# Two transformer blocks on one core: the FFN's norm weight behind the transposes, the modulation blocks placed anew

## The chip, the cores and the metric

The kernel runs on one core of a Trainium2 chip, as one launch. The metric is the device time of that launch in microseconds (us). The core has TensorE (PE, matrix products; its weight loads are listed as PEld), VectorE (DVE), ScalarE (ACT), GpSimd (POOL) and SyncE (SP), each with an instruction queue of its own that is worked through in order, and 16 DMA engines, which SP's and POOL's queues feed here.

## The reference

Two blocks over 256 tokens of width 1024, float32 throughout (cut; the mixers' insides are left out):

```python
def first_block(x, ...):
    h = rms_norm(x, norm_mix_pre)
    proj = h @ w_in
    gates = sigmoid(proj[..., SB_COLS + RW_COLS:] + b_gate)
    o_sb = stick_breaking_attention(q, k, v)
    o_rw = rwkv7_time_mix(p_rw, ...)
    merged = gates[..., :D] * (o_sb @ w_sb_out) + gates[..., D:] * (o_rw @ w_rw_out)
    x = x + rms_norm(merged @ w_o, norm_mix_post)
    h = rms_norm(x, norm_ffn_pre)              # (x * rstd(x)) * norm_ffn_pre
    f = (silu(h @ w_ffn_gate) * (h @ w_ffn_up)) @ w_ffn_down      # d_ff 2816
    return x + rms_norm(f, norm_ffn_post)

def second_block(x, c, ...):
    mod = silu(c) @ w_ada + b_ada                  # w_ada: 1024 x 6144
    sh1, sc1, g1, sh2, sc2, g2 = split(mod, 6)
    h = modulate(x, sh1, sc1)                      # rms_norm(x) * (1 + sc1) + sh1
    u, z, xbc, dt = split(h @ w_in)
    mix = concat([pool_mixer(u, ...), ssd_mixer(z, xbc, dt, ...)]) @ w_out
    x = x + g1 * mix
    h = modulate(x, sh2, sc2)
    x = x + g2 * hier_moe(h, ...)                  # 32 experts, top 2 within a group
    return rms_norm(x) * final_norm_w
```

## The kernel before

Tokens stand in two blocks of 128 (`tb` 0 and 1). Activations that feed a product stand transposed, channels on the 128 partitions, as a pair of float32r tiles: a rounded high part and the rest (`h2Th`, `h2Tl`). Weights are split the same way where they are used: ACT casts the high part (`wh`, L300), DVE subtracts it from the weight (`wl`, L301), and `mm3` (L330 to L332) makes three matmuls of one product. A block of 128 output columns over 1024 inputs (`dense_T`) is 24 matmuls of 256 columns. So each weight costs ACT a cast, DVE a subtraction and PE three matmuls, in that order.

The stages in order, with their place in the profiled span: q, k, v and RWKV's projections (to about 133 us); the gates' products (`pgate`), whose 24-matmul groups stand on PE between the attention's and RWKV's small products (`pwt`, `po`, `pz`; to about 230 us); the two mixers' output products `psb` and `prw`, gated and added into `mTh`/`mTl` (`mg`, L849 to L851); `w_o` with a norm behind it (262 to 304 us); the FFN in 22 groups `g`, each a gate block `pfg` and an up block `pfu` (to 442 us); `w_ffn_down` with two norms behind it (to 518 us); block 2's projection, SSD and pooling, `w_out`, the router (to about 657 us); the experts, whose weights SP streams from memory (to 1107 us).

`dense_rows` makes a product with tokens on the partitions: weights come as row blocks, the last few are kept split, so that token block 0 ends first; then `finish(0)` is written, the kept products of token block 1, `fill()` and `finish(1)`. What `fill` holds is independent PE work for the time in which `finish(1)` is not ready. A scheduler orders the instructions on each engine by its own estimates; the code's `tc.issue_after` can force one behind another. The engines then keep that order.

**The norm at the FFN** (`fin_mix`, L912). POOL makes `gpf` = post-norm weight times FFN-norm weight (L904) and `xgf` = x times FFN-norm weight (L908), ahead of `w_o`'s end. Behind `w_o`, ACT squares the sums `acc` (`sink`, L276), DVE multiplies `acc` by `gpf` (`pn`) and forms the row's reciprocal root in three steps of two small instructions (`rsv`, `rsy`, `rst`; L281 to L288), DVE adds both into `xgf` (L920), PE transposes that (`ptr`, 8 tiles of 128x128), and ACT and DVE take it out as `h2Th` and `h2Tl` in halves of 512 columns. `fin_mix2` makes x itself once more from `acc` (DVE L929, POOL L930), squares it, and PE spreads its reciprocal root over the partitions (`pr`, L933) as `r2`, which scales the FFN's gate products behind them.

**The modulation** `silu(c) @ w_ada` is cut into 24 blocks of 256 columns, 1 MB each, loaded on POOL's queue into two buffers (`wada`). A pair of blocks on PE (`mod_steps`) is 16 `pmod` products (the profile lists such a float32 product as two instructions), a copy of the sums on ACT (`modrow`), four transposes and two small DVE instructions. A block on DVE (`mod_late`) is one multiply and seven multiply-adds of 128x256 (`msum`), two tiny PE products (`pmc`) and an addition. Four pairs stand in the first stage, two in `w_o`'s `fill`, eight blocks on DVE in the FFN (g = 4, 6, ... 18), two pairs in `w_ffn_down`'s `fill`.

**The norms at the projection** (`fin_ffn`, L997): post-norm, addition to x, a second root, x times 1+sc1 (half on DVE, half on POOL), `diag` of the root, and 8 transposes against `diag`, with the shift sh1 added by two products of 512 columns. `fill` there is `router_prep` (L1014): `prb`, the two modulation pairs, `g2h` and `g1row` (rows of modT spread over the partitions, `row_of`, L262).

## Time and profile before

| | us |
|---|---|
| median of 3 runs | 1121.05 |
| lowest and highest | 1119.37, 1121.59 |
| the profiled execution's own time | 1120.24 |
| its span | 1118.5 |
| PE busy | 1053.5 (94%) |
| DVE busy | 592.2 (53%) |
| ACT busy | 403.6 (36%) |
| POOL busy | 82.0 (7%) |

The span is the time between the first and the last instruction of the profiled execution; the times of the runs hold 1.7 us more around it. Busy shares are means over stages with different limits. The chain of work that ended last is PE for 73% of the span, DMA for 15% and DVE for 7%. The clock that TensorE was granted is 0.987 of full speed in the mean.

### The profile page before, as it was taken

The numbers are of one execution on the slowest core, as the hardware profiler recorded it, in microseconds if no ns is written. First come the engines' busy times: TensorE is split into PE (matmuls) and PEld (weight loads), VectorE is DVE, ScalarE is ACT, GpSimd is POOL, SyncE is SP. The second block draws the span as 40 slices with busy tenths as digits, with TensorE's granted clock in tenths as the row PEclk, the third lists the DMA queues.
The fourth block names the chain that finished last, engine by engine and source line by source line (L and its number), as shares of the span: only waits on it lengthen the run. The fifth ranks groups of instructions, "written<-read, shape, count | busy, mean of one in ns | idle before, by whom it ended". The sixth has DMA issues, their size and how long they took to land.

```text
span 1118.5 us, 17553 instructions
## 1 busy us (share of the span) xinstructions
PE 1053.5 (94%) x7022; PEld 732.2 (65%) x7022; DVE 592.2 (53%) x1228; ACT 403.6 (36%) x713; POOL 82.0 (7%) x155
## 2 busy tenths in 40 slices
...
DMA  9654520256566773636664599999999999999993
GB/s 328 219 214 163 193 81 16 101 181 234 196 256 227 263 287 121 253 113 227 247 208 151 184 326 419 410 419 416 416 421 416 415 420 417 416 419 417 417 418 150
DMA packets 57717, 313.01 MB, mean 280 GB/s; under 512 B 8864, under 2 KB 11040, under 8 KB 28064
## 3 DMA queue, kind: packets, MB, share of 16 engines
...
q8 instruction: 57, 0.93, 0.3%
...
## 4 chain that ended last, share of the span: by engine, by line
PE 73%; DMA 15%; DVE 7%; ACT 2%; issue 2%; POOL 1%; SPq 0%; DVEq 0%; POOLq 0%; ACTq 0%
PE ph L1508 15%; DMA wexp<-in_w_dram 11%; PE pyo L1571 7%; PE acc L331 3%; PE acc L332 3%; PE acc L330 3%; PE moe L1589 2%; PE pga L1353 2%; DVE wl L301 2%; PE pfg L330 2%; PE pfg L331 2%; PE pfg L332 2%; PE pfu L331 2%; PE pfu L330 2%; PE pfu L332 2%
## 5 line engine op out<-in xcount | busy, mean ns | idle before, releaser
L1508 PE MATMUL ph<-wexp,xg 128*64 128x512 f32 x1024 | 229.5, 595 | 9.6 <-DMA wexp<-in_w_dram 9.0
L1508 PEld LDWEIGHTS ph<-wexp,xg 128*64 128x64 f32 x1024 | 71.8, 137 | 159.8 <-issue 129.3
L1571 PE MATMUL pyo<-wexp,gy 128*64 128x512 f32 x512 | 116.9, 599 | 2.6 <-DVE gy L1565 2.1
L1515 DVE TENSOR_TENSOR gy<-gy,ph 128x256 f32<-128x256 f32 x32 | 13.5, 421 | 152.2 <-ACT gy L1514 152.2
L1576 DVE SCALAR_TENSOR_TENSOR gy<-pyo,gs,g2h 128x512 f32<-128x512 f32 x32 | 24.0, 751 | 103.5 <-PE pyo L1571 103.5
L1571 PEld LDWEIGHTS pyo<-wexp,gy 128*64 128x64 f32 x512 | 34.1, 137 | 62.5 <-issue 53.7
L1514 ACT ACTIVATE gy<-ph 128x256 f32<-128x256 f32 x32 | 12.3, 383 | 165.0 <-PE ph L1508 165.0
L301 DVE TENSOR_TENSOR wl<-wrows,wh 128x1024 fp32r<-128x1024 f32 (+1 forms) x42 | 51.4, 1241 | 24.9 <-ACT wh L300 24.6
L301 DVE TENSOR_TENSOR wl<-wff,wh 128x1024 fp32r<-128x1024 f32 x44 | 55.1, 1253 | 17.2 <-ACT wh L300 17.1
L1580 ACT CAST yh<-gy 64x512 fp32r<-64x512 f32 x32 | 19.8, 618 | 115.6 <-DVE gy L1576 115.6
L300 ACT CAST wh<-wff 128x1024 fp32r<-128x1024 f32 x44 | 46.0, 1045 | 36.4 <-DMA wff<-in_w_ffn_dram 21.5
L300 ACT CAST wh<-wrows 128x1024 fp32r<-128x1024 f32 (+1 forms) x46 | 45.3, 1009 | 30.5 <-PE acc L331 21.7
L330 PE MATMUL pfg<-h2Th,wh 128*128 128x256 f32 x176 | 50.7, 288 | 0.1
L332 PE MATMUL pfg<-h2Th,wl 128*128 128x256 f32 x176 | 50.0, 284 | 0.0
L331 PE MATMUL pfu<-h2Tl,wh 128*128 128x256 f32 x176 | 49.9, 284 | 0.0
L330 PE MATMUL pfu<-h2Th,wh 128*128 128x256 f32 x176 | 49.9, 284 | 0.0
L332 PE MATMUL pfu<-h2Th,wl 128*128 128x256 f32 x176 | 49.9, 283 | 0.0
L331 PE MATMUL pfg<-h2Tl,wh 128*128 128x256 f32 x176 | 49.9, 283 | 0.0
L1353 PE MATMUL pga<-sel,hnh 128*128 128x256 f32 x128 | 33.1, 305 | 8.7 <-DVE sel L1347 7.0
L332 PE MATMUL pi<-h3Th,wl 128*128 128x256 f32 (+1 forms) x136 | 38.7, 284 | 1.8 <-DVE wl L301 1.8
L331 PE MATMUL pi<-h3Tl,wh 128*128 128x256 f32 (+1 forms) x136 | 38.6, 284 | 0.0
L330 PE MATMUL pi<-h3Th,wh 128*128 128x256 f32 (+1 forms) x136 | 38.6, 284 | 0.0
...
## 6 DMA issues: line engine op xcount, KB each, us to landing
...
```

Of the source, the lines that this page charges most:

```text
L300: act.copy(hi, src)
L301: eng.tensor_tensor(lo, src, hi.bitcast(F32), ALU.subtract)
L330: pe.matmul(ps, lhsT=lh, rhs=rh, start=first, stop=False)
L331: pe.matmul(ps, lhsT=lh, rhs=rl, start=False, stop=False)
L332: pe.matmul(ps, lhsT=ll, rhs=rh, start=False, stop=last)
L1353: return pe.matmul(ps, lhsT=hn[tb][part][:, k * P : (k + 1) * P], rhs=sel[tb].rearrange("p (e j s) -> p e j s", e=GE, j=2)[:, :, 0, :], st ...
L1508: last = pe.matmul(ph_[64 * t_ : 64 * t_ + 64, :], lhsT=xg[k // 4][:, (k % 4) * 256 + el * CAP : (k % 4) * 256 + el * CAP + CAP], rhs=wa[k ...
L1515: dve.tensor_tensor(g, g, ph_[:, 256:512], ALU.mult)
L1571: last = pe.matmul(py_[64 * t_ : 64 * t_ + 64, :], lhsT=gT[:, (kc % 2) * P + (kc // 2) * 64 : (kc % 2) * P + (kc // 2) * 64 + 64], rhs=wb[ ...
L1576: dve.scalar_tensor_tensor(y32, py_, gs, g2h, op0=ALU.mult, op1=ALU.mult)
L1580: act.copy(y[hi], y32[hi])
L1589: last = pe.matmul(acc[tb][hf], lhsT=sT[:, tb * P : (tb + 1) * P], rhs=ys[hf], start=(e == 0), stop=(e == E - 1))
```

## The change

**The FFN's norm weight.** `norm_ffn_pre` is no longer spread over the rows (`gffn`, a DMA on SP's queue); it stands in the table of channel parameters, and multiplies by channel (a scalar of each partition) where the transposes are taken out: ACT writes `h2Th` and DVE `h2Tl` in eight pieces of 128x128 for each token block, in the order `K_TURNS`, which the FFN's products then follow. POOL's five products (`gpf`, four `xgf`) and its four additions to x are gone; `fin_mix` makes x itself in place on DVE, so `fin_mix2` no longer makes it a second time. The 9 matmuls `warm` behind the transposes are gone.

**The order at the FFN's norm.** Three of the FFN's weight splits, of blocks (0,0), (0,1) and (1,0), are written ahead of `finish(0)`; later ones, the root of token block 1 and the first modulation block on DVE are held behind the last piece of `h2Tl` (`behind`).

**The modulation.** One pair moves from `w_o`'s `fill` into the gates' stage; the one that stays there has its products ahead and its sums inside `finish(1)`. The FFN has ten blocks on DVE (g = 3, 5, ... 21) and `w_ffn_down` two (`between`); no pair is left in `router_prep`.

**The norms at the projection.** The squares stand ahead of `pn`; token block 0's transposes are taken out only behind `diag` of token block 1; `prb` and `g2h` are only multiplied in `fill` and taken out behind both norms. `g1row` (8 float32 products of 128x128 and two ACT copies) moves into the SSD stage, behind its last `pys` products.

```diff
-WARM = (16, 4, 5, 2, 9)
+WARM = (16, 4, 5, 2)
+K_TURNS = (0, 4, 1, 5, 2, 6, 3, 7)
...
+    def behind(*ins):
+
+        st = ExitStack()
+        for i in ins:
+            st.enter_context(tc.issue_after(i.ins))
+        return st
...
-    def mod_steps():
+    def mod_products():
...
+
+        def sums():
+            row = small("modrow", [P, 512], bufs=1)
+            act.copy(row, ps)
...
+
+        return sums
+
+    def mod_steps():
+        mod_products()()
...
+        mod_left.append((i, s_))
+
+    def mod_late_sums():
+        while mod_left:
+            i, s_ = mod_left.pop(0)
             ps = psm("pmc")
...
+        if g == 0:
+            mod_steps()
...
+            if between:
+                between(n_)
         for k, hi, lo in kept:
             go(0, k, hi, lo)
+        if ahead:
+            ahead()
         finish(0, acc[0])
...
-    gffn = row_bcast("gffn", a["norm_ffn_pre"])
     h2T = act_T("h2T")
-
-
-    gpf = blk("gpf")
-    pool.tensor_tensor(gpf, gpost, gffn, ALU.mult)
-    xgf = [[hblk("xgf") for _ in range(2)] for _ in range(2)]
-    for tb in range(2):
-        for hf in range(2):
-            pool.tensor_tensor(xgf[tb][hf], halves(xr[tb])[hf], halves(gffn)[hf], ALU.mult)
...
+    def ff_split(g, j):
+
+        if g not in ff_views:
+            t = raw("wff")
+            sync.dma_start(out=t, in_=a["w_ffn"][g])
+            ff_views[g] = [t[:, i * 1024 : i * 1024 + 1024].rearrange("p (k c) -> p k c", k=KC) for i in range(2)]
+        if (g, j) not in ff_parts:
+            ff_parts[g, j] = wsplit(ff_views[g][j], P, (lambda s_: blk(s_, F32R)) if j else None)
+        return ff_parts[g, j]
+
+    def ff_ahead():
+        for gj in ((0, 0), (0, 1), (1, 0)):
+            ff_split(*gj)
...
     def fin_mix(tb, acc):
         t = blk("pn")
-        r = row_rstd(acc, EPS)
+        with behind(*last_split[0]):
+            sums = row_sums(acc)
+            for hf in range(2):
+                dve.tensor_tensor(halves(t)[hf], acc[hf], halves(gpost)[hf], ALU.mult)
+        r = row_rstd_of(sums, EPS)
+        if tb:
+            mod_o.pop()()
         for hf in range(2):
-            dve.tensor_tensor(halves(t)[hf], acc[hf], halves(gpf)[hf], ALU.mult)
-        for hf in range(2):
-            u = xgf[tb][hf]
-            dve.scalar_tensor_tensor(u, halves(t)[hf], r, u, op0=ALU.mult, op1=ALU.add)
-        last = transposed(xgf[tb], None, tb, h2T)
-        if tb:
-            warm(WARM[4], psm("warm"), last)
-        later.append((tb, acc, t, r))
-
-    def fin_mix2(tb, acc, t, r):
-        for hf in range(2):
-            x_, t_ = halves(xr[tb])[hf], halves(t)[hf]
-            dve.scalar_tensor_tensor(t_, acc[hf], r, halves(gpost)[hf], op0=ALU.mult, op1=ALU.mult)
-            pool.tensor_tensor(x_, x_, t_, ALU.add)
+            x_ = halves(xr[tb])[hf]
+            dve.scalar_tensor_tensor(x_, halves(t)[hf], r, x_, op0=ALU.mult, op1=ALU.add)
+        _, pts = transposes(halves(xr[tb]), None)
+        for k in K_TURNS:
+            src = pts[k // 4][:, k % 4 * P : k % 4 * P + P]
+            hi, lo = (atv(h2T[x], k, tb * P, tb * P + P) for x in range(2))
+            h2_done[:] = [act.activation(hi, src, AF.Copy, scale=prm("norm_ffn_pre", k)),
+                          dve.scalar_tensor_tensor(lo, src, prm("norm_ffn_pre", k), hi.bitcast(F32), op0=ALU.mult, op1=ALU.subtract)]
+        later.append(tb)
+
+    def fin_mix2(tb):
         q = row_rstd(halves(xr[tb]), EPS, eps2[:, tb : tb + 1])
         ps = psm("pr2")
         pe.matmul(ps[:, 0:P], lhsT=q.to_broadcast([P, P]), rhs=ident, start=True, stop=True)
         act.copy(r2[:, tb * P : tb * P + P], ps[:, 0:P])
...
-    dense_rows(a["w_o"], KC, mT, fin_mix, SO, keep_o, pos=PO, fill=lambda: [mod_steps() for _ in range(2)])
+    dense_rows(a["w_o"], KC, mT, fin_mix, SO, keep_o, pos=PO, ahead=ff_ahead, fill=lambda: mod_o.append(mod_products()))
...
-    total = None
     for g in range(NF):
-        t = raw("wff")
-        sync.dma_start(out=t, in_=a["w_ffn"][g])
-        vs = [t[:, j * 1024 : j * 1024 + 1024].rearrange("p (k c) -> p k c", k=KC) for j in range(2)]
         p1, p2 = pm("pfg"), pt_("pfu")
-        dense_T(vs[0], KC, h2T, 0, P, p1[:, :256])
-        dense_T(vs[1], KC, h2T, 0, P, p2[:, :256], alloc=lambda s_: blk(s_, F32R))
+        for j, ps in enumerate((p1, p2)):
+            with behind(*h2_done):
+                parts = ff_split(g, j)
+            dense_T(None, KC, h2T, 0, P, ps[:, :256], parts=parts, order=K_TURNS)
         while later:
-            fin_mix2(*later.pop(0))
+            tb = later.pop(0)
+            with behind(*h2_done) if tb else ExitStack():
+                fin_mix2(tb)
...
-        if total:
-            total()
-            total = None
-        if 4 <= g < 20 and g % 2 == 0:
-            total = mod_late(mod_n[0])
-            mod_n[0] += 1
-    if total:
-        total()
+        mod_late_sums()
+        if g > 2 and g % 2:
+            with behind(*h2_done):
+                mod_late()
...
+        sums = row_sums(acc)
         for hf in range(2):
             dve.tensor_tensor(halves(t)[hf], acc[hf], halves(gfp)[hf], ALU.mult)
-        r = row_rstd(acc, eps2[:, tb : tb + 1])
+        r = row_rstd_of(sums, eps2[:, tb : tb + 1])
...
+            last = (dve if XD[hf] else pool).tensor_tensor(halves(t)[hf], halves(xr[tb])[hf], halves(sc1row)[hf], ALU.mult)
+        dg, dg_done = diag(r, True)
+        _, pts = transposes(halves(t), dg, lambda g: modT[:, 4 * g : 4 * g + 4])
+        if tb == 0:
+            held.append(pts)
+        else:
+
+            with behind(dg_done):
+                transposes_out(held[0], 0, h3T)
+            norm_done[:] = last, *transposes_out(pts, 1, h3T)
 
 
...
     def router_prep():
-        ps = psm("prb")
+        mod_late_sums()
+        prb, pg2 = pm("prb"), pm("prow")
         for k in range(KC):
-            pe.matmul(ps[:, 0:40], lhsT=sh2(k).to_broadcast([P, P]), rhs=wrt[:, k], start=(k == 0), stop=(k == KC - 1))
-        dve.tensor_tensor(rbias, rbias, ps[:, 0:40], ALU.add)
-        pool.tensor_tensor(wrt, wrt, sc1p[:, 8:16].rearrange("p (k o) -> p k o", o=1).to_broadcast([P, KC, 40]), ALU.mult)
-        for _ in range(2):
-            mod_steps()
-
-        ps = psm("prow")
+            pe.matmul(prb[:, 0:40], lhsT=sh2(k).to_broadcast([P, P]), rhs=wrt[:, k], start=(k == 0), stop=(k == KC - 1))
+
         for j in range(4):
             for h in range(2):
                 c = 40 + 4 * h + j
-                pe.matmul(ps[64 * h : 64 * h + 64, j * P : (j + 1) * P], lhsT=modT[:, c : c + 1].to_broadcast([P, 64]), rhs=ident, start=True, stop=True)
-        act.copy(g2h, ps)
-        g1.append(row_of("g1row", modT[:, 16:24]))
-
-    dense_rows(a["w_ffn_down"], NF, fT, fin_ffn, SD, lambda s_: blk(s_, F32R), pos=PD, fill=router_prep)
-    g1row = g1[0]
+                pe.matmul(pg2[64 * h : 64 * h + 64, j * P : (j + 1) * P], lhsT=modT[:, c : c + 1].to_broadcast([P, 64]), rhs=ident, start=True, stop=True)
+        prep.extend((prb, pg2))
+
+    def between(n_):
+        mod_late_sums()
+        if n_ in (7, 9):
+            mod_late()
+
+    dense_rows(a["w_ffn_down"], NF, fT, fin_ffn, SD, lambda s_: blk(s_, F32R), pos=PD, fill=router_prep, between=between)
+    with behind(*norm_done):
+        dve.tensor_tensor(rbias, rbias, prep[0][:, 0:40], ALU.add)
+        pool.tensor_tensor(wrt, wrt, sc1p[:, 8:16].rearrange("p (k o) -> p k o", o=1).to_broadcast([P, KC, 40]), ALU.mult)
+        act.copy(g2h, prep[1])
     close_phase()
...
+    g1row = row_of("g1row", modT[:, 16:24])
```

Three places on PE's queue. First the gates' stage (`pgate` is a gate block's products, `pwt`, `po` and `pz` the attention's small products, `ident` the identity that transposes). Before:

```order
L330 MATMUL pgate336_2279<-hTh4_143,wh337_2280 128x256
L331 MATMUL pgate336_2279<-hTl6_145,wh337_2280 128x256
L332 MATMUL pgate336_2279<-hTh4_143,wl338_2281 128x256
L822 MATMUL pwt284_2067<-ident_96,sg282_2061 128x128 x3
L825 MATMUL po272_2031<-wT283_2062,vtok209_1588 64x256
L826 MATMUL po272_2031<-wT283_2062,vtok209_1588 64x128
L811 MATMUL pz287_2079<-kaT208_1587,qT207_1586 128x128
L812 MATMUL pz287_2079<-kaT208_1587,qT207_1586 128x256
```

After:

```order
L349 MATMUL pgate332_2247<-hTl6_145,wh333_2248 128x256
L350 MATMUL pgate332_2247<-hTh4_143,wl334_2249 128x256
L410 MATMUL pmod335_2277<-wada336_2278,csil_140 32x256 x8
L410 MATMUL pmod335_2277<-wada337_2288,csil_140 32x256 x8
L416 MATMUL pmod335_2277<-ident_96,modrow338_2298 128x128 x4
L855 MATMUL pwt284_2067<-ident_96,sg282_2061 128x128 x3
L348 MATMUL pgate341_2309<-hTh3_142,wh342_2310 128x256
L349 MATMUL pgate341_2309<-hTl5_144,wh342_2310 128x256
```

A pair's 16 products and 4 transposes now stand ahead of `pwt`, and the 24 products of the gate block that stood there come behind it.

Second, PE behind the last product of `w_o`. Before:

```order
L389 MATMUL pmod491_3237<-wada492_3238,csil_140 32x256 x8
L389 MATMUL pmod491_3237<-wada493_3248,csil_140 32x256 x8
L393 MATMUL pmod491_3237<-ident_96,modrow494_3258 128x128 x4
L389 MATMUL pmod496_3267<-wada497_3268,csil_140 32x256 x8
L319 MATMUL ptr507_3318<-ident_96,xgf457_3055 128x128 x4
L389 MATMUL pmod496_3267<-wada498_3278,csil_140 32x256 x8
L319 MATMUL ptr508_3325<-ident_96,xgf458_3056 128x128 x4
L369 MATMUL warm509_3332<-ident_96 128x128
L393 MATMUL pmod496_3267<-ident_96,modrow499_3288 128x128 x4
L369 MATMUL warm509_3332<-ident_96 128x128 x8
L330 MATMUL pfg511_3365<-h2Th450_3047,wh513_3367 128x256
```

After:

```order
L410 MATMUL pmod498_3283<-wada499_3284,csil_140 32x256 x8
L410 MATMUL pmod498_3283<-wada500_3294,csil_140 32x256 x8
L416 MATMUL pmod498_3283<-ident_96,modrow507_3323 128x128 x4
L325 MATMUL ptr509_3334<-ident_96,x2_87 128x128 x4
L325 MATMUL ptr510_3339<-ident_96,x2_87 128x128 x4
L348 MATMUL pfg511_3381<-h2Th454_3075,wh483_3186 128x256
```

One pair's products and its transposes stand ahead of token block 1's transposes, which read x in place of `xgf`; the second pair and `warm` are gone, and the FFN's first product follows at once.

Third, PE behind the last product of `w_ffn_down` (`diag828` and `diag820` are token block 1's; `pi` is the projection). Before:

```order
L1029 MATMUL prow813_5520<-ident_96,modT_141 64x128
L262 MATMUL prow815_5531<-ident_96,modT_141 128x128 x4
L262 MATMUL prow816_5537<-ident_96,modT_141 128x128 x4
L315 MATMUL ptr829_5584<-modT_141,ident_96 128x512
L389 MATMUL pmod808_5490<-wada810_5501,csil_140 32x256 x8
L321 MATMUL ptr829_5584<-diag828_5582,pn817_5543 128x128 x4
L393 MATMUL pmod808_5490<-ident_96,modrow811_5511 128x128 x4
L315 MATMUL ptr830_5592<-modT_141,ident_96 128x512
L321 MATMUL ptr830_5592<-diag828_5582,pn817_5543 128x128
L1029 MATMUL prow813_5520<-ident_96,modT_141 64x128 x7
L321 MATMUL ptr830_5592<-diag828_5582,pn817_5543 128x128 x3
L330 MATMUL pi2839_5662<-h3Th723_4996,wh840_5663 128x256
```

After:

```order
L1078 MATMUL prb807_5499<-wrt_5007,modT_141 128x40 x5
L327 MATMUL ptr805_5463<-diag804_5461,pn793_5422 128x128 x4
L327 MATMUL ptr806_5469<-diag804_5461,pn793_5422 128x128 x4
L1078 MATMUL prb807_5499<-wrt_5007,modT_141 128x40 x3
L1083 MATMUL prow808_5500<-ident_96,modT_141 64x128 x8
L321 MATMUL ptr821_5558<-modT_141,ident_96 128x512
L321 MATMUL ptr822_5564<-modT_141,ident_96 128x512
L327 MATMUL ptr821_5558<-diag820_5556,pn809_5517 128x128 x4
L327 MATMUL ptr822_5564<-diag820_5556,pn809_5517 128x128 x4
L348 MATMUL pi2831_5643<-h3Th721_5016,wh832_5644 128x256
```

Both pairs and `g1row` (`prow815`, `prow816`) are gone; `prb` and `g2h` (`prow808`) stand around token block 0's transposes, and those of token block 1 come last.

## Rows read from the trace of the kernel before

**Rows 1.** the page: mean busy tenths of the DMA engines, 40 slices of the span

```profile
DMA  9654520256566773636664599999999999999993
```

**Rows 2.** windows: us; busy us of PE, PEld, DVE, ACT, POOL; granted clock; DMA share; GB/s

```profile
150.00:180.00 30.00, 29.98 (x462) 24.59 (x461) 18.92 (x34) 13.10 (x25) 0.96 (x1) 0.92 0.10 37
258.00:264.00 6.00, 3.81 (x14) 3.02 (x15) 6.00 (x7) 1.97 (x3) 6.00 (x4) 0.72 0.93 356
360.00:390.00 30.00, 30.00 (x253) 30.00 (x252) 25.29 (x47) 13.89 (x20) 1.59 (x3) 1.00 0.70 253
506.00:510.00 4.00, 2.23 (x26) 1.08 (x23) 3.82 (x10) 1.93 (x5) 1.79 (x2) 1.00 0.92 340
602.00:614.00 12.00, 12.00 (x66) 9.41 (x65) 7.79 (x22) 9.47 (x28) 0.00 (x0) 1.00 0.40 133
690.00:700.00 10.00, 9.48 (x48) 3.88 (x49) 4.51 (x8) 1.86 (x4) 0.00 (x0) 1.00 1.01 421
```

**Rows 3.** timeline of DVE: start, us, engine line op, out<-in [idle <-releaser]

```profile
251.70 1.23 DVE L301 TENSOR_TENSOR wl<-wrows,wh 128x1024 fp32r<-128x1024 f32 x1
...
255.04 3.42 DVE L301 TENSOR_TENSOR wl<-wrows,wh 128x1024 fp32r<-128x1024 f32 x1
...
258.72 1.42 DVE L301 TENSOR_TENSOR wl<-wrw,wh 128x512 fp32r<-128x512 f32 x1
...
263.69 1.51 DVE L301 TENSOR_TENSOR mTl<-mg,mTh 128x256 fp32r<-128x256 f32 x1
```

**Rows 4.** timeline of POOL around w_o

```profile
257.34 7.58 POOL L908 TENSOR_TENSOR xgf<-x,gffn 128x512 f32<-128x512 f32 x4
...
288.97 0.59 POOL L385 DMA_DIRECT2D wada<-in_w_ada_dram  x1 [2.94 <-PE pmod L389]
```

**Rows 5.** timeline of PE from the gates to the FFN's start

```profile
146.27 0.52 PE L822 MATMUL pwt<-ident,sg 128*128 128x128 f32 x3 [1.08 <-DVE zinv L611]
...
260.19 0.45 PE L332 MATMUL prw<-orw_h,wl 128*128 128x256 f32 x1 [3.28 <-DVE wl L301]
...
287.45 1.93 PE L389 MATMUL pmod<-wada,csil 128*32 128x256 f32 x32
...
294.38 1.88 PE L389 MATMUL pmod<-wada,csil 128*32 128x256 f32 x16 [3.10 <-DMA wada<-in_w_ada_dram]
...
299.46 1.07 PE L389 MATMUL pmod<-wada,csil 128*32 128x256 f32 x16 [1.91 <-DMA wada<-in_w_ada_dram]
...
303.81 0.39 PE L330 MATMUL pfg<-h2Th,wh 128*128 128x256 f32 x1
...
311.56 0.49 PE L933 MATMUL pr<-ident,rsy 128*128 128x128 f32 x2 [0.91 <-DVE rsy L288]
```

**Rows 6.** timeline of ACT at the FFN's norm

```profile
277.24 0.60 ACT L276 ACTIVATE sink<-acc 128x512 bf16<-128x512 f32 x1 [4.56 <-PE acc L332]
...
299.24 1.04 ACT L300 CAST wh<-wff 128x1024 fp32r<-128x1024 f32 x1 [5.55 <-DMA wff<-in_w_ffn_dram]
```

**Rows 7.** timeline of DVE at both norms and at block 2's w_out

```profile
281.26 1.41 DVE L920 SCALAR_TENSOR_TENSOR xgf<-pn,rsy,xgf 128x512 f32<-128x512 f32 x2
...
505.57 1.28 DVE L326 TENSOR_TENSOR h3Tl<-ptr,h3Th 128x512 fp32r<-128x512 f32 x2
...
511.39 0.29 DVE L295 TENSOR_SCALAR diag<-ident,rsy 128x128 f32<-128x128 f32 x1
...
620.09 0.35 DVE L1287 SCALAR_TENSOR_TENSOR mixTl<-pyt,par,mixTh 128x128 fp32r<-128x128 f32 x1
```

**Rows 8.** timeline of PE from ffn_down to the projection

```profile
499.90 1.87 PE L1019 MATMUL prb<-wrt,modT 128*128 128x40 f32 x16
...
508.58 1.07 PE L389 MATMUL pmod<-wada,csil 128*32 128x256 f32 x16 [1.07 <-DMA wada<-in_w_ada_dram]
...
509.95 2.05 PE L262 MATMUL prow<-ident,modT 128*128 128x128 f32 x16
...
518.13 0.37 PE L330 MATMUL pi<-h3Th,wh 128*128 128x256 f32 x1
```

65 lines of the change are left out of this document (38 added, 27 removed).

## The prediction

> **What bounds the kernel now.** I read the slices first. From slice 24 on, the experts, the DMA engines are full [rows 1], and a window there shows a share of 1.01 at 421 GB/s [rows 2]. Ahead of it they stand mostly between 2 and 7 tenths. The bytes of the experts are fixed, and their stream begins when buffers come free, that is when compute ahead has got there. So a microsecond saved ahead of slice 23 (about 645 us) should arrive at the end, and inside the experts PE has nothing to give. Ahead of it PE is the bound: windows in the gates, in the FFN and in the SSD stage show it busy for 29.98 of 30, 30.00 of 30 and 12.00 of 12 us [rows 2]. What is left are the seams where it is not: behind the mixers' outputs PE has 3.81 of 6 us, at the second norm 2.23 of 4 [rows 2]. The PE timeline says what it waits for at them: `wl` on DVE for 3.28 us at 260.19, `wada` transfers for 3.10 and 1.91 us at the FFN's norm [rows 5] and for 1.07 us at the projection [rows 8]. The change works at just these three seams and pays with PE work put into two full stages. I add five terms, each the shift of the work behind it.
>
> **Term 1, the gates: 2.3 us lost (0 to 4).** A pair costs PE 1.93 us of products [rows 5] and four transposes of 128x128, about 0.5 by 2.05 for sixteen instructions of that size [rows 8]; the ACT copy between them lets PE wait some 0.7 to 1.2 us, since nothing is queued between. That is about 3.4 us. Ahead of `pwt` it takes the place of 24 gate products: 253 take 30 us in a full window [rows 2], so 24 take 2.85. `pwt` waited for `zinv` from DVE for 1.08 us [rows 5] and is thus released by DVE, not by what stands ahead, so it still starts near 146.3. The 2.85 us come behind it instead; five of these products (0.6) now fill the wait for `pwt`'s copy. Loss 2.85 - 0.6 = 2.25. If the ACT copy stands behind other ACT work, `pwt` starts late too: up to 4. If the shifted work keeps PE busy where its clock fell (0.92 in the mean of the window from 150 [rows 2], 2.4 us of it), nothing is lost.
>
> **Term 2, mixers' outputs: 4.4 us gained (3 to 5.5).** POOL's `xgf` products run from 257.34 for 7.58 us [rows 4], behind `gpf`. Beside POOL's products the same DVE subtraction takes 3.42 us that took 1.23 just before [rows 3]; `wl<-wrw` takes 1.42 (half the columns, so some 0.6 alone); five DVE instructions are stretched so, from 255.04 to 263.69 [rows 3]. PE's 3.28 us at 260.19 end with the second of them. Without POOL both give back 2.2 + 0.8 = 3.0 us, so PE goes on at 257.2. After the pause the granted clock was 0.72 in the mean of the window, so most of the 3.81 busy us ran at 1.2 in place of 2.4 GHz [rows 2]: 1.0 to 1.9 us more, of which I take 1.7. Sum 4.7; 0.3 goes again, as token block 0's transposes now wait for x itself, made on DVE from the earlier sum.
>
> The Trainium skill ("SBUF — State Buffer", section "SBUF: two separate sides", on the port pair that VectorE and GpSimd share) says that a DVE instruction with two SBUF inputs and a GpSimd instruction shut each other out for a whole instruction. The trace agrees in that the subtraction with both inputs in SBUF nearly trebles. By that rule alone DVE could lose all of POOL's time, 7.58 us and `gpf`'s; the sum does not use it, since the stretched rows hold less.
>
> **Term 3, the FFN's norm: 6.5 us gained (4.5 to 8.5).** Before, the last sum ends near 287.4 and the first FFN product stands at 303.81 [rows 5], 16.4 us on. Between them the second pair's two transfers, issued by POOL from 288.97 only [rows 4], hold PE twice, and an ACT cast of weights that waits 5.55 us for its transfer stands ahead of `h2Th` [rows 6]. Now one pair is left, whose blocks were loaded long before, and no cast stands in between. What remains is the chain of the norm. Token block 0's chain, undisturbed, took from the first square at 277.24 [rows 6] to the end of `xgf` at 281.26 + 1.41 [rows 7], 5.4 us. To this come 0.6 us for the pair's small DVE work, 1.0 for 8 transposes and 0.7 for the first channel's piece on ACT and on DVE (0.35 [rows 7]): 7.7 us. The other pieces, 8 x 0.35 = 2.8 us on DVE, keep just ahead of PE, which needs three products of 0.12 for each.
> The 8.7 us so gained are not all kept. The gate's scale `r2` needs both roots, and behind `h2Tl` DVE has two chains of about 4 us (277.24 to 281.26) and three weight subtractions of 1.23: the end of `h2Tl` at 9.3, then 11 us at most in part beside each other, so `pr` of token block 1 near 20.3 us after the sum. In the order about 75 products stand ahead of it. Before, it came 24.4 us after the sum (311.56 + 0.2) with 53 products done, by the timeline's count. The gain is 24.4 - 20.3 = 4.1 us, and 22 products more by then, 22 x 0.12 = 2.6: 6.7, of which I keep 6.5. If the chain ends later the bound is 4.5; if PE is never held there, 8.5.
>
> **The FFN itself: 0.** A group takes 48 products, 5.7 us by the full window. DVE was busy for 25.29 of those 30 us with a modulation block in every second group [rows 2], 4.8 us for a group, and it has the same density after; there are two groups more of it, and two blocks in `w_ffn_down`. PE's cover is that it waits for none of this as long as DVE stays under 5.7.
>
> **Term 4, the norms at the projection: 5.0 us gained (3 to 6.5).** Before, 499.90 to 518.13 is 18.2 us [rows 8]. DVE had `diag` of token block 1 ready at 511.39 + 0.29, 11.8 us after the sum [rows 7], and PE was the late one: two pairs with a transfer of their own, and 2.05 us of `g1row` [rows 8]. Now `fill` is `prb` and `g2h` alone, PE waits for `diag`, and DVE becomes the chain: without `h2Tl`'s counterpart of token block 0 (1.28 us, now behind `diag`) and the pairs' small work (0.7) it ends at 11.8 - 2.0 = 9.8. Transposes 1.0 and the first half's way out 0.6 make 11.4, gain 6.8. But PE has then little to do for 4 us and more, which cost half the clock for a stretch at 260; I take off 1.5 for that and 0.3 for `g2h` and other late ACT work. In the window from 506, with 2.23 of 4 us busy, the clock stayed at 1.00 [rows 2], so this 1.5 lies between 0 and 3.
>
> **Term 5, `g1row` in the SSD stage: 2.0 us lost (0.5 to 2.5).** 2.05 us of PE [rows 8], where PE is full (12.00 of 12 us [rows 2]). A pause just behind it would hide some.
>
> POOL's queue loses its additions to x and so issues `wada` sooner; SP's loses one small load. Each is free while the experts' buffers set the stream.
>
> **Sum.** -2.3 + 4.4 + 6.5 + 0 + 5.0 - 2.0 = 11.6 us. The profiled execution took 1120.24; 1120.24 - 11.6 = 1108.6. The median of the runs is 0.8 above it: 1109.4.
>
> **The rivals.**
> *The clock falls at both norms.* PE pauses for some 5 us ahead of the FFN and again ahead of the projection, and the products that stood there as cover (the pairs, `warm`) are gone. The window at 258 shows a fall after 3.28 us of waiting; the one at 506 shows none. If each stage starts at half clock for 3 to 4 us, each loses a further 1.5 to 2, and a late `pr` takes 2 more, 5.5 in all: 1109.4 + 5.5 = 1115.
> The Trainium skill ("TensorE: Matmul & The Clock Gate", section "HAM oscillation — how this bites in real kernels") has such pauses re-throttle the array each time, at half clock afterwards. By that rule this rival is the forecast, with 1115; the 506 window, half idle at full clock, speaks against taking it everywhere.
> *More comes free.* The gates lose nothing, `g1row` is half hidden, and the clock holds: +2.3 + 1.0 + 1.5 + 1.0 gives 17.4, so 1103.6.
> *It does not reach the end.* If the experts' stream is bound by transfers that start at a fixed point, the seams only lengthen the wait there: about 1121. For it speaks that the last 450 us are DMA at 1.01. Against it, the engines stand far from full ahead of slice 23, so that buffers and not bytes set the start.
> *Slower: DVE bounds the FFN.* Place: each of 22 groups. DVE takes 4.8 of 5.7 us. The forced orders could put modulation pieces ahead of a `wl` that PE needs at once. Price: 22 times what DVE's turn exceeds 5.7. It decides at 11.6 / 22 = 0.53 us over, a turn of 6.2; a turn of 6.6 costs 22 x 0.9 = 19.8, so 1109.4 + 19.8 = 1129. The full window with 30.00 of 30 at the same density speaks against it.
>
> **How the numbers follow.** A measurement of this kernel can tell about 0.2%, 2.2 us, from no change. Forecast 1106 to 1112.5: 0.50. More comes free: 0.15. Clock falls (1112.5 to 1118.5): 0.20. Not reaching the end: 0.07. Slower: 0.08, DVE or another queue. Faster 0.85, same 0.07, slower 0.08. The range 1102 to 1117 takes in the sums of the low and the high ends as far as these cases reach; beyond it lie the last two cases and the edges of the others, 0.2 in all.
>
> **What would show it.** At 255 `wl<-wrows` takes 1.2 us and PE's 3.28 us idle is gone. The first `pfg` stands 7 to 9 us behind the last `acc`, and the wait at the second `pr` or at the first `ffs` is 1 to 3 us. The first `pi` stands 11 to 13 us behind the sum, released by `diag`. The gates end about 2.3 us later, `z`'s sum 2 us later than the shift. PE stays at 30 of 30 in the FFN. A wait of PE for `wl<-wff` in every group, or `ph` starting no earlier, would make it wrong.

## The result, and the profile after

The changed kernel takes **1104.12 us** (median of 4 runs, 1103.91 to 1105.53) against 1121.32 us for the kernel before on the same chip (4 runs, 1119.37 to 1122.65): ratio **0.9859**, 95% interval 0.9844 to 0.9873. It is faster by 17.2 us, where 11.6 were forecast. The profiled execution took 1104.01 us with a span of 1102.3.

The page of the kernel after, mean busy tenths of the DMA engines in 40 slices:

```profile
DMA  9554540347466785527454699999999999999993
```

As in [rows 1], the slices at the end are full, 16 of the last 17. Their stretch did not change: from the first expert product `ph` to the end of the span it is 461.1 us in both traces. So the whole gain lies ahead of `ph`, and all of it arrived. I cut the PE timeline at the same instructions in both traces; `w_o`'s products are taken to end where the first `pmod` behind them starts. "Behind the sum" counts from there below, and at the projection from the first `prb`. The third column is worked out from the first two.

| stretch on PE | before, us | after, us | gained |
|---|---|---|---|
| start to first `pgate` | 133.76 | 132.31 | +1.45 |
| gates: to first `psb` | 99.16 | 99.73 | -0.57 |
| mixers' outputs: to the end of `w_o`'s products | 54.53 | 48.93 | +5.60 |
| FFN's norm: to first `pfg` | 16.36 | 9.26 | +7.10 |
| FFN: to the last group's last `pfg` | 128.94 | 130.44 | -1.50 |
| `w_ffn_down`: to `prb` | 67.15 | 68.09 | -0.94 |
| projection's norm: to first `pi` | 18.23 | 11.33 | +6.90 |
| projection and SSD: to first `ph` | 139.26 | 141.10 | -1.84 |
| experts | 461.1 | 461.1 | 0.0 |

The sum is 16.2 us, the difference of the two spans (1118.5 and 1102.3).

Windows of the kernel after, at the places of [rows 2] (columns as there: busy us of PE, PEld, DVE, ACT, POOL, then clock, DMA share, GB/s):

```profile
258.00:264.00 6.00, 6.00 (x28) 4.91 (x27) 5.14 (x8) 4.42 (x6) 0.00 (x0) 1.00 1.00 419
288.00:294.00 6.00, 3.77 (x18) 3.80 (x19) 4.73 (x16) 4.48 (x11) 0.00 (x0) 0.55 0.70 294
348.00:378.00 30.00, 30.00 (x253) 30.00 (x253) 23.98 (x46) 12.73 (x19) 1.06 (x2) 1.00 0.71 258
492.00:498.00 6.00, 3.51 (x26) 1.98 (x25) 5.20 (x18) 1.92 (x5) 2.32 (x2) 1.00 0.00 0
```

Behind the mixers' outputs PE is now busy for 6.00 of 6 us at full clock; in [rows 2] it was 3.81 at 0.72. In the FFN it is full at 30.00 of 30 with DVE at 23.98, as before. At the two norms it still pauses, and the two pauses end differently: the FFN's begins at a clock of 0.55, the projection's keeps 1.00 although PE has only 3.51 of 6 us there.

DVE of the kernel after, the instructions of [rows 3] and the pieces of `h2Tl` at the FFN's norm:

```profile
254.04 1.22 DVE L302 TENSOR_TENSOR wl<-wrows,wh 128x1024 fp32r<-128x1024 f32 x1
...
255.51 0.68 DVE L302 TENSOR_TENSOR wl<-wrw,wh 128x512 fp32r<-128x512 f32 x1
...
257.91 0.41 DVE L302 TENSOR_TENSOR mTl<-mg,mTh 128x256 fp32r<-128x256 f32 x1
...
286.64 0.35 DVE L977 SCALAR_TENSOR_TENSOR h2Tl<-ptr,par,h2Th 128x128 fp32r<-128x128 f32 x1
...
289.73 0.35 DVE L977 SCALAR_TENSOR_TENSOR h2Tl<-ptr,par,h2Th 128x128 fp32r<-128x128 f32 x1 [0.18 <-ACT h2Th L976]
```

The subtraction that took 3.42 us in [rows 3] takes 1.22, that of half the columns 0.68 in place of 1.42, and that of a quarter (`mTl`) 0.41 in place of 1.51. POOL has nothing there any more.

PE of the kernel after, behind the mixers, at the FFN's norm, in `w_ffn_down` and at the projection's norm, the places of [rows 5, 8] (start, us, instruction, count, in brackets the wait ahead and its releaser):

```profile
256.24 0.39 PE L350 MATMUL prw<-orw_h,wl 128*128 128x256 f32 x1 [0.34 <-DVE wl L302]
...
280.97 1.93 PE L410 MATMUL pmod<-wada,csil 128*32 128x256 f32 x32
283.90 0.66 PE L416 MATMUL pmod<-ident,modrow 128*128 128x128 f32 x4 [0.99 <-ACT modrow L414]
285.55 1.39 PE L325 MATMUL ptr<-ident,x 128*128 128x128 f32 x8 [1.00 <-DVE x L971]
290.23 0.55 PE L348 MATMUL pfg<-h2Th,wh 128*128 128x256 f32 x1 [3.29 <-DVE h2Tl L977]
290.58 0.41 PE L349 MATMUL pfg<-h2Tl,wh 128*128 128x256 f32 x1
290.79 0.41 PE L350 MATMUL pfg<-h2Th,wl 128*128 128x256 f32 x1
...
301.78 0.38 PE L983 MATMUL pr<-ident,rsy 128*128 128x128 f32 x2
...
430.93 0.50 PE L447 MATMUL pmc<-onec,msum 128*128 128x1 f32 x4
...
498.26 2.05 PE L327 MATMUL ptr<-diag,pn 128*128 128x128 f32 x16 [2.75 <-DVE diag L296]
500.09 0.50 PE L348 MATMUL pi<-h3Th,wh 128*128 128x256 f32 x2
```

The wait for `wl` at `prw` has shrunk from 3.28 us to 0.34. At the FFN's norm no transfer holds PE. It waits 0.99 us for the pair's copy, 1.00 for x, and then 3.29 for `h2Tl`, and behind that its products stand 0.21 us apart (290.58, 290.79), where the full clock gives 0.12. `pr` of token block 1 stands at 301.78, 20.8 us behind the sum. The row at 430.93 is one of the sums of modulation blocks in `w_ffn_down`. Ahead of the projection's first product `pi` the only wait is 2.75 us for `diag`.

### The profile page after: what moved, and what is told of

Its sections match the earlier page's. It is cut to its first block, busy times and chain, and to the rows that moved or that the text cites. A ratio compares the mean times of both kernels' runs of the same rounds, so it can differ in the third digit from the quotient of the medians.

```text
span 1102.3 us, 17424 instructions
## 1 busy us (share of the span) xinstructions
PE 1041.2 (94%) x6948; PEld 726.8 (66%) x6948; DVE 597.0 (54%) x1268; ACT 406.1 (37%) x723; POOL 66.9 (6%) x146
## 4 chain that ended last, share of the span: by engine, by line
PE 74%; DMA 13%; DVE 8%; ACT 2%; issue 1%; POOL 1%; SPq 0%; DVEq 0%; ACTq 0%; POOLq 0%
PE ph L1570 15%; DMA wexp<-in_w_dram 11%; PE pyo L1633 8%; PE acc L349 3%; PE acc L350 3%; PE acc L348 3%; PE moe L1651 2%; PE pga L1415 2%; PE pfg L348 2%; PE pfg L349 2%; PE pfg L350 2%; PE pfu L349 2%; PE pfu L348 2%; PE pfu L350 2%; DVE wl L302 2%; PE prw L350 1%
## 5 line engine op out<-in xcount | busy, mean ns | idle before, releaser
L1633 PEld LDWEIGHTS pyo<-wexp,gy 128*64 128x64 f32 x512 | 34.1, 136 | 62.5 <-issue 54.8
L302 DVE TENSOR_TENSOR wl<-wrows,wh 128x1024 fp32r<-128x1024 f32 (+1 forms) x42 | 48.5, 1170 | 20.9 <-ACT wh L301 20.7
L439 DVE SCALAR_TENSOR_TENSOR msum<-wada,csil,msum 128x256 f32<-128x256 f32 x84 | 40.3, 480 | 1.2
```

The lines of the kernel that those rows point to most:

```text
L302: return h, eng.tensor_tensor(lo, src, hi.bitcast(F32), ALU.subtract)
L439: dve.scalar_tensor_tensor(s_, v[:, k], csil[:, k : k + 1], s_, op0=ALU.mult, op1=ALU.add)
L1633: last = pe.matmul(py_[64 * t_ : 64 * t_ + 64, :], lhsT=gT[:, (kc % 2) * P + (kc // 2) * 64 : (kc % 2) * P + (kc // 2) * 64 + 64], rhs=wb[ ...
```

## Experiments

The ratio is to the kernel before on the same chip. Its medians were 1119.78 us beside e0 to e3, 1120.28 beside c0 and e4 to e6, and 1120.46 beside e7 to e10. The last column compares with the change itself: the ratio less 0.9860 (the mean of its two measurements), times 1120 us. By the intervals it is uncertain by some 2 us, for e7, e9 and e10 by 3 to 4, so that the traces have to decide what is smaller.

| run | median, us | ratio (95%) | against the change, us |
|---|---|---|---|
| the change itself | 1104.12 | 0.9859 (0.9844 to 0.9873) |  |
| c0, the change again | 1105.20 | 0.9862 (0.9843 to 0.9882) |  |
| e1, POOL's products back | 1109.43 | 0.9900 (0.9882 to 0.9917) | +4.5 |
| e2, no pair in the gates | 1102.54 | 0.9841 (0.9826 to 0.9857) | -2.1 |
| e3, `g1row` in the fill | 1102.44 | 0.9838 (0.9822 to 0.9853) | -2.5 |
| e4, PSUM layout earlier | 1106.61 | 0.9877 (0.9861 to 0.9894) | +1.9 |
| e5, PSUM layout later | 1101.04 | 0.9831 (0.9814 to 0.9848) | -3.2 |
| e6, products as cover | 1105.67 | 0.9874 (0.9856 to 0.9891) | +1.6 |
| e7, e3 and e5 together | 1099.01 | 0.9811 (0.9787 to 0.9834) | -5.5 |
| e8, before with one pair in the gates | 1119.13 | 0.9987 (0.9972 to 1.0003) | +14.2 |
| e9, two pairs back at the projection | 1108.44 | 0.9905 (0.9872 to 0.9938) | +5.0 |
| e10, the gates' pair back at the FFN's norm | 1107.68 | 0.9889 (0.9860 to 0.9917) | +3.2 |

**Both kernels once more.** e0 is the kernel before unchanged (one run, 1119.62 us), c0 the kernel after.

> The kernel before, unchanged, profiled once more. Asked: does the half clock in its first third belong to its order of work, or to the single execution? Before showed a granted clock of 0.77 from 124 to 130 us and 0.50 from 148 to 154, after showed 1.00 in both. If the order of work makes it, this run shows about 0.77 and 0.50 again and a span near 1118.5. If it is a matter of the execution, one of the two stands at 1.00 and the span is 1.5 to 3 us shorter or the stretch lies elsewhere.

> The kernel after, unchanged, on the same chip as the three runs beside it. Expected ratio to before 0.986 as in its first runs, some 16 us less. For the clock: if the missing half clock between 124 and 154 us belongs to the order of work, the windows 124 to 130 and 148 to 154 stand at 1.00 again; if it was chance, one of them stands lower and the ratio is nearer 0.988.

The question was whether the clock falls in the same places each time. Windows of e0, then of c0, in the stretch ahead of the gates, in the gates, and at the FFN's norm:

```profile
124.00:130.00 6.00, 4.41 (x13) 3.51 (x14) 5.79 (x11) 1.00 (x2) 5.29 (x10) 0.74 0.83 328
148.00:154.00 6.00, 6.00 (x25) 5.02 (x24) 4.48 (x7) 2.42 (x6) 0.00 (x0) 0.50 0.08 31
```

```profile
124.00:130.00 6.00, 4.02 (x17) 3.05 (x18) 5.79 (x11) 1.58 (x2) 5.29 (x10) 1.00 0.88 344
148.00:154.00 6.00, 5.57 (x44) 5.06 (x43) 5.41 (x8) 2.89 (x6) 0.96 (x1) 1.00 0.76 321
288.00:294.00 6.00, 3.22 (x15) 3.25 (x16) 4.84 (x14) 4.87 (x12) 0.00 (x0) 0.55 0.79 326
```

The kernel before repeats its two half-speed stretches (0.77 and 0.50 in its first trace, 0.74 and 0.50 here). The kernel after repeats that it has none there, and that it has one at the FFN's norm (0.55 both times).

**POOL's products (e1).** The products that the change took off POOL run again there, into tiles that nobody reads.

```diff
     h2T = act_T("h2T")
+    gpf = blk("gpf")
+    pool.tensor_tensor(gpf, gpost, gpost, ALU.mult)
+    xgf = [[hblk("xgf") for _ in range(2)] for _ in range(2)]
+    for tb in range(2):
+        for hf in range(2):
+            pool.tensor_tensor(xgf[tb][hf], halves(xr[tb])[hf], halves(gpost)[hf], ALU.mult)
```

> The kernel after with five products on GpSimd put back where before had them (128x1024 and four of 128x512, of x and the post-norm's row), their results not used; the rest as after. Theory (term 2): DVE's subtractions beside them stretch to 3 us and more again, PE waits some 3 us for the one of the last prw, its clock falls, and 4.4 to 5.6 us are lost: 1108.5 to 1109.7. Rival: the products only lie in DVE's slack and the gain of that stretch came from the order of w_o's splits: within 1 us of 1104.1.

From the first `psb` to the end of `w_o` it takes 54.8 us, as before (54.53), against 48.9 in the kernel after. POOL and DVE of e1 there:

```profile
252.63 1.93 POOL L940 TENSOR_TENSOR gpf<-gpost 128x1024 f32<-128x1024 f32 x1 [100.10 <-DMA gpost<-in_norm_mix_post_dram]
254.53 6.20 POOL L944 TENSOR_TENSOR xgf<-x,gpost 128x512 f32<-128x512 f32 x4
```

```profile
251.59 1.23 DVE L302 TENSOR_TENSOR wl<-wrows,wh 128x1024 fp32r<-128x1024 f32 x1 [0.15 <-ACT wh L301]
...
254.77 1.75 DVE L302 TENSOR_TENSOR wl<-wrw,wh 128x512 fp32r<-128x512 f32 x1
256.44 0.41 DVE L884 TENSOR_TENSOR mg<-psb,gate 128x256 f32<-128x256 f32 x1
...
259.53 2.29 DVE L302 TENSOR_TENSOR wl<-wrows,wh 128x1024 fp32r<-128x1024 f32 x1
261.74 0.41 DVE L885 TENSOR_TENSOR mg<-prw,gate 128x256 f32<-128x256 f32 x1
```

While POOL works, `wl` of 128x512 takes 1.75 us (0.68 in the kernel after) and of 128x1024 2.29 (1.23 just ahead). PE of e1 then waits 2.59 us for `wl` at 256.57, and the clock is 0.77 and 0.66 in the windows from 252 and from 258. So POOL's products alone, though nothing needs them, bring back the whole loss of this stage: 54.8 - 48.9 = 5.9 us, where the change had gained 5.6. The instruction that reads PSUM for one of its inputs, `mg<-psb,gate`, takes 0.41 us in the same stretch and the same 0.41 at 261.74, when POOL was done. The Trainium skill ("SBUF — State Buffer", section "SBUF: two separate sides") ties the exclusion to DVE instructions in a two-port mode or with two SBUF inputs; the trace agrees in who is stretched (2.29 against 1.23) and who is not (0.41).

**The gates' pair (e2, e10).** e2 leaves the pair out (its two blocks, four columns of modT, are set to zero). e10 puts it back where before had a second one, behind `w_o`.

```diff
         if g == 0:
-            mod_steps()
+            mod_n[0] += 2
+            pool.memset(modT[:, 16:20], 0.0)
```

> The kernel after with the modulation pair in the gates' stage left out (its two loads, 16 products, four transposes; its four columns of modT are set to zero, so this part of the modulation is not computed). The prediction's term 1: PE's queue is 2.3 us shorter there, so 1101.8. Rival: the pair's products kept PE's clock up where before fell to 0.50 (148 to 154 us); without them the half clock is back and takes 2 to 3 us, so 1104 to 1105, with a granted clock well under 1.00 in some window of 142 to 160.

From the first `pgate` to `psb` it takes 98.3 us against 99.7: the pair costs 1.5. PE of e2 in that stage:

```profile
147.40 0.52 PE L855 MATMUL pwt<-ident,sg 128*128 128x128 f32 x3 [1.08 <-DVE zinv L644]
148.49 0.65 PE L858 MATMUL po<-wT,vtok 128*64 128x256 f32 x2 [0.57 <-ACT wT L856]
```

These are the waits of the kernel before ([rows 5]: 1.08 us for `zinv`), and yet the clock was 1.00 from 148 to 154, where before had 0.50. The rival that PE's pause at `pwt` makes the clock fall, and that the pair helps by filling it, falls with this row.

```diff
-        if g == 0:
-            mod_steps()
...
-    dense_rows(a["w_o"], ..., fill=lambda: mod_o.append(mod_products()))
+    dense_rows(a["w_o"], ..., fill=lambda: (mod_steps(), mod_o.append(mod_products())))
```

> The kernel after with the gates' modulation pair back at the FFN's norm, where two pairs then follow each other. By the prediction's terms the gates give 2.3 us back and the norm loses what the second pair's transfers cost, 5 us of PE's waits before: 2 to 3 us slower than after, 1106.5 to 1107. Rival: the transfers fall into the wait for x and h2Tl that PE has there anyway (5.3 us in after), so only the pair's own 2.5 us count and the gates pay them back: within 1 us of after.

PE of e10 behind `w_o`:

```profile
288.88 1.94 PE L410 MATMUL pmod<-wada,csil 128*32 128x256 f32 x16 [0.55 <-DMA wada<-in_w_ada_dram]
...
293.69 0.58 PE L348 MATMUL pfg<-h2Th,wh 128*128 128x256 f32 x1 [0.34 <-DVE mods L418]
```

The gates get 1.5 us back, in agreement with e2, and the FFN's norm grows from 9.3 to 14.1 us behind the sum, at a clock of 0.50 and 0.60 in the windows from 288 and from 294. The whole is some 3 us slower than the kernel after (4.8 - 1.5 = 3.3 in the trace). So moving the second pair away is worth some 5 us at the norm for 1.5 at the gates.

**The pair moved alone (e8).** The same move, done in the kernel before with all else left as it was.

```diff
+        if g == 0:
+            mod_steps()
...
-    dense_rows(a["w_o"], ..., fill=lambda: [mod_steps() for _ in range(2)])
+    dense_rows(a["w_o"], ..., fill=mod_steps)
```

> The kernel BEFORE with one part of the change alone: one of the two modulation pairs of w_o's fill stands in the gates' stage instead. At the FFN's norm the waits for wada (3.10 and 1.91 us) go, but the chain of the norm and the ACT cast of weights that waits for its transfer stay: there 2 to 5 us gained. In the gates: by the prediction 2.3 us lost; if the pair's products keep the clock up between 147 and 154 us, nothing is lost there (granted clock 1.00, where both profiles of before show 0.50), and the whole is 1116 to 1118. If the clock falls there all the same, the pair is not what keeps it in after: 1118 to 1121.

It is not measurably faster. PE of e8 at the FFN's norm, then windows ahead of the gates and in the gates:

```profile
297.66 1.97 PE L319 MATMUL ptr<-ident,xgf 128*128 128x128 f32 x8 [5.15 <-DVE xgf L922]
...
303.52 0.41 PE L330 MATMUL pfg<-h2Th,wh 128*128 128x256 f32 x1
```

```profile
124.00:130.00 6.00, 3.91 (x17) 2.66 (x15) 5.78 (x11) 1.74 (x2) 5.43 (x9) 1.00 0.97 360
148.00:154.00 6.00, 5.57 (x43) 4.84 (x41) 5.40 (x8) 2.64 (x6) 0.96 (x1) 1.00 0.89 375
```

The waits for `wada` [rows 5] are gone, and a wait of 5.15 us for `xgf` has come in their place: between the steps of the root DVE still has four subtractions of weights, 1.2 us each, as in the kernel before, and ends `xgf` no earlier. The first `pfg` stands at 303.52, before at 303.81. The pair's move pays only with the rest of the change. What at this norm belongs to the order of the weights' splits and what to the norm weight's new place was not taken apart. The windows show a clock of 1.00 at 124 and at 148, in a kernel whose PE order is that of before up to 142 us.

**The PSUM layout at the FFN (e4, e5).** My step "the first `pfg` waits for the first channel's piece only" is tested here. In the kernel after, `pfg` waited until 290.08, when the last of the eight `h2Tl` pieces (289.73, 0.35 us) was done; the first had been done at 286.99. The line ahead of the FFN, `open_banks(4, 0, 4)`, lays PSUM out anew. e4 moves it ahead of `w_o`, e5 behind the FFN's groups.

```diff
     mod_o = []
 
+    open_banks(4, 0, 4)
+
     def keep_o(s_):
...
-    open_banks(4, 0, 4)
     open_phase("ffn")
```

> The kernel after, but the PSUM banks are laid out anew ahead of w_o in place of behind it. In after the first pfg started at 290.23, 0.15 us behind the LAST of the eight pieces of h2Tl, though it reads the first. Theory: it waited for the new layout's bank, which comes free only when everything of the old layout has been read; with the layout changed earlier the first pfg waits for its own piece and stands 2.5 to 3 us sooner behind the last acc, about 6.5 us on. What of it reaches the end: 1 to 3 us, since the first ffs waits for r2 (302.7 in after) and four banks hold just two groups. Rival: the wait is for the whole h2T tile and nothing moves; or the new layout ahead of w_o costs there what it saves later (the last prw and psb have to be read first): within 1 us of after.

PE of e4:

```profile
261.56 0.47 PE L348 MATMUL acc<-wh,mTh 128*128 128x512 f32 x1 [1.11 <-ACT wh L301]
...
291.24 0.56 PE L348 MATMUL pfg<-h2Th,wh 128*128 128x256 f32 x1
...
305.00 0.49 PE L983 MATMUL pr<-ident,rsy 128*128 128x128 f32 x2 [1.03 <-DVE rsy L289]
306.86 0.58 PE L348 MATMUL pfg<-h2Th,wh 128*128 128x256 f32 x1 [1.38 <-DVE ffs L1015]
```

```diff
-    open_banks(4, 0, 4)
     open_phase("ffn")
...
+    open_banks(4, 0, 4)
     gfp = row_bcast("gfp", a["norm_ffn_post"])
```

> The kernel after, but the PSUM banks are laid out anew behind the FFN, ahead of w_ffn_down, so that the FFN works with five banks for its products in place of four. Theory as for the early layout: the first pfg stands about 6.5 us behind the last acc. With five banks PE can go on half a group longer before the first ffs, so more of it is kept: 2 to 4 us less than after. Rival: the new layout's wait moves to the first acc of w_ffn_down, which then stands behind the last f: 0 to 1 us less, with an idle PE there of 1 to 3 us.

PE of e5:

```profile
288.01 0.56 PE L348 MATMUL pfg<-h2Th,wh 128*128 128x256 f32 x1
...
302.23 0.38 PE L983 MATMUL pr<-ident,rsy 128*128 128x128 f32 x2
...
421.12 2.05 PE L263 MATMUL prow<-ident,sc1p 128*128 128x128 f32 x16 [0.70 <-DVE ffs L1015]
```

In both, `pfg` comes right behind the transposes, without a wait: 6.5 and 6.4 us behind the start of `w_o`'s last product, against 9.6 in the kernel after. Nothing else was moved, so it is the new layout at this place that made PE wait for all the pieces. That it is the reuse of the old layout's banks, which `ptr` filled and `h2Tl` reads, fits; it was not taken apart further.

What e4 wins it gives back: a wait of 1.11 us for `wh` at the layout's new place, 1.03 at `pr`, and 1.38 at the `pfg` behind it, two groups (96 products) in, released by `ffs`, with a clock of 0.72 in the window from 306. e5 keeps the old layout through the FFN: `pr` of token block 1 comes at 302.23 with 108 products done ahead of it, against 301.78 and 75 in the kernel after, and PE waits nowhere from 288 to 421, although the clock falls at the norm here too (0.81 in the window from 288). The FFN's norm and the FFN together (last `acc` to last `pfg`) take 135.6 us against 140.0, 4.4 less. `w_ffn_down` gives 1.1 of it back (69.2 us to `prb` against 68.1): the new layout now stands ahead of it, and PE waits 0.70 us there for the last `ffs`. So the traces show 3.3 us for the layout's place. The median is 4.2 lower than that of the kernel after on the same chip (c0), 3.2 by the ratios; e5's profiled execution holds 1.5 us more in its favour, from the clock in block 2's `w_out` (see e3). e4's time holds one thing more: its first `pgate` stood at 135.7, 3.4 us later than in the kernel after, with a clock of 0.92 and 0.79 in the windows from 124 and from 130, though the code there is the same.

**Products as cover at the FFN's norm (e6).** Fourteen products of nothing stand behind token block 1's transposes, so that PE does not pause.

```diff
-        _, pts = transposes(halves(xr[tb]), None)
+        last, pts = transposes(halves(xr[tb]), None)
+        if tb:
+            warm(14, psm("warm"), last)
```

> The kernel after with 14 warm products of 128x128 (float32, unused) behind token block 1's transposes at the FFN's norm; in after PE waits 3.29 us there and the FFN's first 24 products then run at half clock (0.21 us apart, not 0.12), 2.2 us lost. Theory: with PE busy in the wait the clock holds, and the first ffs, which waits for r2 near 302.7, comes at most 1 us sooner, so 0 to 2 us less than after. Rival: the clock falls all the same, as it did at 294.5 in before behind a wait of 3.10 us: no gain, and up to 0.5 us lost, if the warm products end later than the last piece of h2Tl.

PE of e6, and the window:

```profile
287.58 3.29 PE L390 MATMUL warm<-ident 128*128 128x128 f32 x28
291.04 0.36 PE L348 MATMUL pfg<-h2Th,wh 128*128 128x256 f32 x1 [0.17 <-DVE h2Tl L979]
...
300.99 0.49 PE L985 MATMUL pr<-ident,rsy 128*128 128x128 f32 x2 [0.63 <-DVE rsy L289]
```

```profile
288.00:294.00 6.00, 5.83 (x51) 5.67 (x51) 4.73 (x13) 5.14 (x13) 0.00 (x0) 1.00 0.82 337
```

The wait falls from 3.29 to 0.17 us and the clock stays at 1.00 (0.55 in the kernel after), so the pause does cost the clock there. Of the 2.2 us that the half clock takes (24 products at 0.21 in place of 0.12 us) the trace gives back 1.4: the last `pfg` stands 138.3 us behind the sum against 139.7. The chain of `r2` is then the next late thing, `pr` waits 0.63 us for `rsy`. The medians on this chip (1105.67 against 1105.20 of c0) do not show the 1.4 us, and by their intervals they can't exclude it.

**`g1row` (e3).** It goes back from the SSD stage to `router_prep`'s fill, with nothing else.

```diff
-        prep.extend((prb, pg2))
+        prep.extend((prb, pg2, row_of("g1row", modT[:, 16:24])))
...
-    g1row = row_of("g1row", modT[:, 16:24])
```

> The kernel after with g1row's 8 float32 products back in w_ffn_down's fill, behind g2h's. In after, PE waits 2.75 us there for diag of token block 1. Theory: the 2.05 us of g1row fit into that wait, and the SSD stage gets its 1.4 us back: 1102.7. Rival: ACT's two copies of g1row (0.6 each) stand ahead of the copies of h3Th, or the products push the transposes of token block 1 past diag, and what the SSD stage gains is lost ahead of the projection: 1104 to 1105.

PE of e3 at the projection's norm:

```profile
494.98 2.05 PE L263 MATMUL prow<-ident,modT 128*128 128x128 f32 x16
...
499.77 2.05 PE L327 MATMUL ptr<-diag,pn 128*128 128x128 f32 x16 [0.73 <-DVE diag L296]
```

The 2.05 us now lie in the wait for `diag`, which falls from 2.75 to 0.73 us; the norm takes 11.4 us as without it, and the stretch from `pi` to `ph` 138.2 in place of 141.1, 2.9 less. The comparison of whole times has 2.5. But only 1.4 us of this lie where `g1row` stood: from the first `pdt` to the first `pyt` of the SSD stage it is 46.9 us against 48.3. The other 1.5 lie behind `pyt`, in block 2's `w_out`. There the kernel after runs at half clock for some 3 us, in both of its traces (and so does the kernel before), and e3 does not. Nor does e5, which has `g1row` where the kernel after has it and the same waits. Windows of the kernel after, then of e5, each from 6 us behind the first `pyt`:

```profile
606.13:609.13 3.00, 3.00 (x9) 2.33 (x8) 2.32 (x9) 0.19 (x1) 0.00 (x0) 0.50 0.98 377
```

```profile
603.79:606.79 3.00, 3.00 (x15) 2.37 (x14) 2.32 (x9) 0.19 (x1) 0.00 (x0) 1.00 0.91 358
```

So 1.4 us are shown for `g1row`; that the clock held behind it may be chance.

**Both together (e7).** e3's and e5's edits in one kernel.

> The kernel after with two of the tried edits together: the PSUM banks laid out anew behind the FFN (ratio 0.9831 to before alone, against 0.9862 for after), and g1row back in w_ffn_down's fill (0.9838 alone, against 0.9859). They touch different stages, so if both gains are real they add: 3.5 + 2 us, ratio 0.981, near 1099. Rival: g1row's gain was within the spread of the runs (intervals of 1.7 us each way): ratio 0.983, as the late banks alone.

1099.01 us, by the ratio 5.5 under the kernel after; the two alone gave 3.2 and 2.5. The rows at both places are those of e5 and e3 (the wait for `diag` is 0.73 us again). In the traces the way from the first `pgate` to `ph` is 6.1 us shorter than in the kernel after; 1.5 of these are again the clock in `w_out`. This beats both kernels.

**Two pairs back at the projection's norm (e9).** Four of the twelve blocks on DVE, those that the change gave to it, go back to PE, in two pairs, in `router_prep`.

```diff
-        if g > 2 and g % 2:
+        if 4 < g < 20 and g % 2:
...
+        for _ in range(2):
+            mod_steps()
...
-        if n_ in (7, 9):
-            mod_late()
```

> The kernel after with the two last modulation pairs back in w_ffn_down's fill (eight blocks on DVE in the FFN, none in w_ffn_down), as before had them; the norms' order and g1row stay as in after. Theory (term 4): the second pair's transfers are issued only when the first pair's products are done and land over 5 us later, so PE's transposes for token block 1 or the first products behind them wait for it: 4 to 6 us lost, 1108 to 1110. Rival: the gain of that seam came from g1row's leaving and from the order of the norm, and the pairs hide behind the wait for diag: under 2 us lost.

PE of e9:

```profile
492.29 1.93 PE L410 MATMUL pmod<-wada,csil 128*32 128x256 f32 x32
...
498.57 0.94 PE L327 MATMUL ptr<-diag,pn 128*128 128x128 f32 x6 [1.99 <-DVE diag L296]
499.43 1.07 PE L410 MATMUL pmod<-wada,csil 128*32 128x256 f32 x16
...
503.00 1.07 PE L410 MATMUL pmod<-wada,csil 128*32 128x256 f32 x16
```

From `prb` to the first `pdt` behind the projection it takes 68.3 us against 63.1, 5.2 more; the FFN and `w_ffn_down`, with fewer blocks on DVE, give 1.4 of it back in the trace. By the ratio the whole is 5.0 slower. The size came as expected, but not the way: no wait for a transfer stands there. The first pair fits ahead of the wait for `diag`; the second pair's products, two groups of 1.07 us at 499.43 and 503.00, lie behind it and among the first `pi`, where PE has other work to do.

## Why the prediction came out as it did

The direction and the place of every gain that was forecast were right: the three seams gave 5.6, 5.6 and 6.9 us, the end received the whole shift, and the FFN did not become DVE's. Two of the five terms lay within 1 us of the traces, the other three 1.2 to 1.9 off, all of them to the low side. The sum was 4.6 us short in the spans (16.2 against 11.6). About half of these 4.6, 1.45 ahead of the gates and 0.9 in them, are half-speed stretches that the kernel before had and the kernel after had not; the sum has no term for them, and why they are gone is open, so this part of the gain was not foreseen.

**Term 1, the gates (forecast -2.3).** Measured -0.57 in the stage, and the pair itself costs 1.5 (e2, e10). So the term's own price was set 0.8 too high: I counted the displaced products but for five at full length, and which more of them came free was not traced. The other 0.9 is the clock: the kernel before ran at 0.50 from 148 to 154, in both of its traces, and the kernel after at 1.00; e2, with no pair, before's waits and full clock, is 0.9 us shorter there than the kernel before. I had allowed for this in one sentence, as the low end of the loss. The +1.45 us ahead of the gates, where before had a clock of 0.77 and after 1.00, was not forecast at all. Why these stretches are gone stays **open**. It is not the wait at `pwt` nor the pair: e2 and e10 have before's waits of 1.08 and 0.57 us and a clock of 1.00. PE's order ahead does not decide it either: e8 has before's order up to 142 us and 1.00, and e4 has after's order and fell to 0.92 and 0.79.

**Term 2, the mixers' outputs (+4.4).** Measured 5.6. The mechanism is shown by e1, which takes all of it back by POOL's products alone. The direct part was sized exactly: from `psb` to the `prw` that waited is 27.27 us before and 24.20 after, 3.1 us where I had 3.0. From that `prw` to the end of `w_o` it is 27.26 and 24.73, 2.5 us where I took 1.7 for the clock. The clock itself was sized right: from that `prw` to the fourth `acc` product, where the half speed ends, it is 3.63 us before and 1.99 after, 1.6 of the 2.5. The other 0.9 lie behind, at full clock, mostly in short gaps ahead of `acc` products. That DVE was still working off its stretched instructions then (1.51 us for `mTl` at 263.69 [rows 3]) fits, and was not taken apart; the sum had no term for it.

**Term 3, the FFN's norm (+6.5).** Measured 7.1 up to the first `pfg` and -1.5 in the FFN, together 5.6. One step was wrong: the first `pfg` did not wait for its own piece alone, but for all of them (3.29 us), and began at 9.3 us behind the sum in place of 7.7 (without that wait it is 6.2 in e4 and 6.1 in e5). PE fell to half clock there. Neither hurt the sum as much as it might, because I had made the sum by `pr`, at 20.3 us with some 75 products ahead of it; it came at 20.8 with 75, and without the wait of 1 to 3 us that was forecast there, since PE was late by itself. (The 9.3 us taken for the end of `h2Tl` do not follow from the terms beside them, which give 10.2; it came at 9.1.) e6 shows the rest: with the clock kept, the last `pfg` comes 1.4 us sooner and the next late thing is that same chain. e5 shows what the wrong step was worth once PE has banks to run ahead: 33 more products by `pr`, 33 x 0.12 = 4.0 us, and 0.5 us by which `pr` came earlier, 4.5 in all, where the trace has 140.0 - 135.6 = 4.4.

**The FFN and `w_ffn_down` (0).** Nearly 0 in the FFN apart from the above, PE at 30.00 of 30 and no wait for `wl`; nine sums of blocks stand on PE's queue there, where before had eight. In `w_ffn_down` it is -0.94: three such sums stand there (the row at 430.93 is one) where before had none, 0.94 / 3 = 0.3 us each; e9, with none there, has 67.2 us as before. I had counted the blocks' cost on DVE and none on PE.

**Term 4, the projection's norm (+5.0).** The chain by `diag` gave 6.8 us, and 6.9 were measured; the first `pi` stands 11.3 us behind the sum, where I had 11.4. The deduction of 1.5 for the clock was wrong: PE paused for 2.75 us and kept 1.00 in the windows from 492 and from 498. [Rows 2] with 2.23 of 4 us at 1.00 had said so, and I weighed it less than the fall at 258. The price is not always nil: in e2, behind the same wait of 2.75 us, the window from 498 has 0.72, and `pi` came 12.1 us behind the sum.

**Term 5, `g1row` (-2.0).** Measured -1.84 from `pi` to `ph`, of which 1.4 lie between the first `pdt` and the first `pyt`, where `g1row` stands, and 0.4 ahead of them, in the projection, which was not followed up. So the size came near in part by luck. e3 shows that the move was not needed: the wait for `diag` that term 4 leaves would have hidden it, and its stage gets 1.4 us back (2.9 with the clock in `w_out`). I had worked out this wait ("PE has then little to do for 4 us and more") without asking which of the moved work would fit in it.

**The rivals.** The forecast of a clock that falls at both norms did not come: it fell at the FFN's (0.55, which cost 1.4 us up to the FFN's end by e6) and held at the projection's. The Trainium skill ("TensorE: Matmul & The Clock Gate", section "HAM oscillation — how this bites in real kernels") tells of waits for data behind which the array starts at half clock, every time anew. The traces here agree behind the wait of 3.29 us, in both traces of the kernel after; behind 2.75 us the clock held there and fell in e2. "More comes free" (1103.6) is nearest to what happened: the gates lost 0.57, the clock held at the projection, though `g1row` was not hidden. The slower case, DVE bounding the FFN, is excluded by 30.00 of 30, and the case that it does not reach the end by `ph`, 16.2 us earlier with 461.1 us behind it in both.
